# The opening of a two-layer Fourier and attention kernel: another order of its loads, turns and sine steps, written out by hand

## The chip, the cores and the metric

One core of a Trainium2 chip runs the whole program, all in fp32. The metric is device time in microseconds (us): the median of three runs of the kernel before is 1846.85 us (1846.19 to 1848.97). A profiled execution, from which every other number here comes, took 1846.4 us.

The engines are named as in the profile: PE is TensorE, DVE is VectorE, ACT is ScalarE, POOL is GpSimd, and SP is the engine whose queue issues most loads. Each engine works through its own instructions in a fixed order and waits at semaphores.

## The reference

Two layers on 256 tokens and 256 context tokens of width 2048. Both layers modulate a normalised input by vectors that come from a matrix product with `ada_w`. The first layer is a Fourier mixer with 16 groups of 256 channels:

```python
shift, scale, gate = jnp.split((jax.nn.silu(c) @ ada_w[i] + ada_b[i])[:, None, :], 3, axis=-1)
h = _rmsnorm(x, norm_g[i]) * (1 + scale) + shift
...
u, z = jnp.split(h @ w_in, 2, axis=-1)
ug = u.reshape(b, n, FNET_GROUPS, FNET_GROUP_DIM).astype(jnp.float32)
f = jnp.fft.fft2(ug, axes=(1, 3), norm='ortho').real.astype(h.dtype)
f = jnp.einsum('bngc,gcd->bngd', f, w_mix).reshape(b, n, D_BRANCH)
return f * jax.nn.silu(z)
...
x = x + gate * (y @ w_out[i])
```

The second layer is windowed attention with context keys and a sink, then a last norm. The change touches the first layer's opening alone.

## The kernel before

The kernel takes the Fourier transform over the tokens first, on the raw input, and multiplies by `w_in` afterwards. So the opening, roughly the first 130 us, has three strands of work:

- **Transform steps** (`x_split`, `dft_unit`, `evac_dft`): the 16 column blocks k of the input, 128 columns each, times cosine and sine tables. Each gives a tile `hx[k]`, which must then be scaled by the modulation (`scale_hx`, DVE line 286 and ACT line 285) and get its first column repaired (`fix_f0`), before it can be used.
- **Ada tiles** (`ada_tile`, PE line 213): 32 loads of 1 MiB, `awp`, each worth 8 matmuls in the trace. Four tiles make one row block: shift or scale for a quarter of the columns (four column blocks k). Its rows are copied out by ACT (`ada_rows`, line 218), and turned by four PE transposes, the "turns" (`ada_fin`, line 225), after which DVE adds the bias and stores shift or scale. Tiles 0 to 3 give the scale of the first quarter, 4 to 7 its shift, and so on to tile 31, the last shift.
- **Fill steps** (`fill_pe`, `u_step`, `sp_step`): products of the weights `wu` with the scaled `hx`, for groups 0, 1 and 2. The weights of a group come in two halves kh of 1 MiB, for column blocks 0 to 7 and 8 to 15. A half is folded by DVE into a difference (`m`, the sine part) and a sum (`p`, the cosine part); each is split into a high and a low number (ACT casts, line 62; DVE subtracts, line 63), since fp32 products are made of three matmuls (`mm3`, lines 75 to 77). A step (g, nm, k) is three matmuls; "s" is a product for two single columns of every group. The list `fill` fixes the order of the steps, `fill_pe(n)` takes the next n of them. Sine steps need no repaired column, cosine steps do.

Loads go through SP's queue, in the order of the program, into a few buffers (`raw_st` hands them out: three named raw, two raw2, two raw3); a load is issued when the matmuls or the fold that used its buffer before are done. Smaller loads go through ACT's queue. The third group's halves (g = 2) are loaded by `load_uh(2, kh, ...)` into raw2 buffers and folded by `fold_2`: the difference at line 463, the sum, in place, at line 460.

PE's order is chained by hand with `pe_next()`: what stands under it is issued behind the last matmul named `pe_end`. `tc.issue_after(x)` holds other work back to behind instruction x. What is not chained is ordered by a scheduler when the program is built. Before the change, a loop `for p in range(8, 12)` with `opening_step(p)` placed tiles 16 to 23 (two a step), and the tail, from `ada_tile(24)` on, was written out.

Within the loop `for g in range(G)` that follows (lines 535 to 616), PE goes on with group 0's mixing and then the groups up to 15.

Of the kernel before, what the change touches and what calls it, by code (L numbers as in the profile page):

```python
# [10 lines left out]
F32 = mybir.dt.float32  # L11
# [5 lines left out]
P = 128  # L17
D = 2048
KT = D // P
# [9 lines left out]
def tile_dit(ctx: ExitStack, tc: tile.TileContext, a: dict, out: bass.AP):  # L29
# [133 lines left out]
    with tc.tile_pool(name="st", reuse_waits="tile", bufs=1, side="right") as st:  # L163
# [111 lines left out]
            V.tensor_copy(f0[:, k, :], o[:, 0::N])  # L275
            hx.append(r)

        scale_end = [None]

        def scale_hx(k):  # L280
            r = hx[k]
            h, l = act(F32R), act(F32R)
            for s in range(2):
                q = slice(s * N, (s + 1) * N)
                S.activation(h[:, q], r[:, q], AF.Copy, scale=gs0[:, k, s : s + 1])
                scale_end[0] = V.scalar_tensor_tensor(l[:, q], r[:, q], gs0[:, k, s : s + 1], h[:, q].bitcast(F32), op0=ALU.mult, op1=ALU.subtract).ins
            hx[k] = (h.rearrange("p (s j) -> p s j", s=2), l.rearrange("p (s j) -> p s j", s=2))

# [27 lines left out]
        for g, nm, k in ((0, "m", 0), (0, "p", 0), (0, "m", 4), (1, "m", 0), (1, "p", 0), (1, "m", 4), (0, "p", 4), (1, "p", 4), (0, "s", 0), (0, "s", 4), (0, "m", 8), (1, "m", 8), (0, "p", 8), (1, "p", 8), (0, "s", 8), (2, "m", 0), (2, "m", 4), (0, "m", 12), (1, "m", 12), (2, "m", 8), (2, "m", 12), (2, "p", 0), (2, "p", 4), (2, "p", 8), (0, "p", 12), (0, "s", 12), (1, "p", 12), (2, "p", 12)):  # L316
# [11 lines left out]
        fills = {7: (8, 4), 11: (4, 0)}  # L328

        def opening_step(p):  # L330
            nb, which = p // 4, 1 - p // 2 % 2
            if p == 0:
                x_split(0)
            if p == 1:
                x_split(1)
            if p in (2, 4):
                x_split(p // 2 + 1, (0,))
            us_ = units.get(p, ())
            fl = fills.get(p, (4, 4))
            if p < 2:  # L340
# [30 lines left out]
            for k in range(KT):  # L371
                if max(k // 4 * 4 + 2, k // 2) == p:
                    scale_hx(k)
            if p % 4 == 0 and p:
                fix_f0(p // 4 - 1)

        uload = {4: (0, 0), 6: (1, 0), 7: (0, 1), 9: (1, 1)}
        uhold = {(0, 0): 4.9, (1, 0): 6.9, (0, 1): 7.9, (1, 1): 9.9}
        for p in range(5):
            opening_step(p)  # L380
        sta.close()
# [4 lines left out]
            wu[0][0] = split_uh(*raws[0, 0])  # L386
        opening_step(6)
        raws[1, 0] = fold_uh(raws[1, 0], 1, 0)
        opening_step(7)
        with tc.issue_after(rows_end[0]):  # L390
            wu[1][0] = split_uh(*raws[1, 0])
        del ring[5:]
        std.close()

# [26 lines left out]
            m_end[1] = V.scalar_tensor_tensor(sp[64:96, :], o2[64:96, 0:GD], mk[64:96, g : g + 1], sp[64:96, :].bitcast(F32), op0=ALU.mult, op1=ALU.subtract).ins  # L421
            return pqh, pql, sp

        for p in range(8, 12):
            if p == 8:
                cst = ua.tile([P, 4, P], F32, name="cst", bufs=1)
                nc.scalar.dma_start(cst, a["cst"])
                ch = ua.tile([P, 4, P], F32R, name="ch", bufs=1)
                cl = ua.tile([P, 4, P], F32R, name="cl", bufs=1)
                mk = cload("mk", [96, G], nc.scalar, adap)  # L430
                wsr = wsp.tile([P, 512], F32, tag="ws", name="wsr")
                nc.scalar.dma_start(wsr, a["wsp"])
            opening_step(p)
            if p == 9:
                split(ch, cl, cst)
                spw = wsp.tile([P, 1024], F32R, tag="ws", name="spw")
                sph, spl = spw[:, 0:512], spw[:, 512:1024]
                split(sph, spl, wsr)
                with pe_next(), tc.issue_after(f0_end[0]):
                    m0 = load_m(0)  # L440
            if p == 11:
                with pe_next():
                    m1 = load_m(1)
            for kh, q in ((0, 8), (1, 10)):
                if p == q:
                    raws[kh, 1] = fold_uh(raws[kh, 1], kh, 1)
                if p == q + 1:
                    with tc.issue_after(rows_end[0]):
                        wu[kh][1] = split_uh(*raws[kh, 1])

        def split_ws(nm, t):
            l = wsp.tile([P, 8, 127], F32R, tag="ws", name=f"w{nm}l")
# [4 lines left out]
        def fold_2(kh, nm):  # L457
# [5 lines left out]
            V.tensor_tensor(m, v[:, :, 0, :], v[:, :, 1, :], op=ALU.subtract)  # L463
            wu[2][kh]["m"] = split_ws("m", m)

        ada_tile(24)
        ada_tile(25)
# [903 lines left out]
```

## Time and profile before

| what | number |
|---|---|
| median of three runs | 1846.85 us |
| profiled execution | 1846.4 us, span from first to last instruction 1844.5 us |
| PE busy | 1812.6 us of the span |
| DVE, ACT busy | 1395.3 us, 958.1 us |
| DMA | 366.37 MB, 199 GB/s on the mean |
| loads of `awp` | 32 of 1 MiB, median 13.0 us from issue to landing |
| loads of `wu` | 32 of 1016 KB, median 8.0 us from issue to landing |

How to read the views that follow. A row of the stretches gives the window, its length, then the busy time of PE, PE's weight loads, DVE, ACT and POOL with counts, the granted TensorE clock, the mean busy share of the DMA engines and GB/s. A row of the timeline gives the start, the duration, engine, line, operation, output and inputs with buffer numbers left out, shapes, and how many like it were merged; in brackets the idle time before it and what ended it. A row of the waits gives who waited for whom: total us, times, longest. In DMA rows the queue of the issuing engine is named, SPq for example.

### The profile page before, as it was taken

To read this page: it belongs to the slowest core of one execution; us is meant where nothing else is said; L and a number is where in the kernel's file an instruction comes from. 1 tells how busy PE (TensorE), PEld (TensorE's weight loads), DVE (VectorE), ACT (ScalarE), POOL (GpSimd) and SP (SyncE) were. 2 spreads that over 40 slices of the span, in tenths; PEclk is the share of its full clock that TensorE was granted. 3 is DMA by queue.
4 is the path that set the end of the run, shared out by engine and by line. 5 is a ranking of instruction groups with operands and counts; after the bars stand their busy time and mean duration, and the time that the engine had idled before them with its cause. 6 is when DMAs were issued, how large, how long until landed. Compare 5 with 4: busy or idle time off the path is not lost.

```text
span 1844.5 us, 26534 instructions
## 1 busy us (share of the span) xinstructions
PE 1812.6 (98%) x9917; PEld 1548.5 (84%) x9917; DVE 1395.3 (76%) x2777; ACT 958.1 (52%) x1662; POOL 173.8 (9%) x185
## 2 busy tenths in 40 slices
PE   6999999999999999999999999999999999999997
PEld 5689999888888888888888888888888888888886
DVE  5688888787878887858874836878878878887455
ACT  5444444432222242214222625888888888897343
POOL 0001212000000000000000001121220220300001
PEclk9999999999999999999999999999999999999999
DMA  9988889666666648553575324333333333444553
GB/s 394 417 314 233 222 232 275 225 226 224 243 244 262 235 169 294 214 214 114 206 286 208 115 95 156 123 130 138 115 117 135 135 117 137 160 138 179 186 182 137
DMA packets 74593, 366.37 MB, mean 199 GB/s; under 512 B 21153, under 2 KB 21809, under 8 KB 39393
## 3 DMA queue, kind: packets, MB, share of 16 engines
q1 hardware_dynamic: 50400, 326.67, 48.2%
q0 software_dynamic: 19920, 31.06, 6.6%
q10 hardware_dynamic: 4144, 6.95, 1.2%
q8 instruction: 78, 1.28, 0.3%
q14 instruction: 51, 0.41, 0.1%
HBM read 352.06 MB, written 12.59 MB: 198 GB/s over the span
## 4 chain that ended last, share of the span: by engine, by line
PE 93%; DMA 3%; DVE 2%; ACT 1%; issue 1%; POOL 0%; POOLq 0%; SPq 0%; ACTq 0%; DVEq 0%
PE ps L75 24%; PE ps L76 24%; PE ps L77 24%; PE ps L1052 6%; PE ps L1054 3%; PE ps L1108 3%; DMA raw<-in_awp 2%; PE ps L1123 2%; PE ps L1122 2%; PE ps L1088 2%; PE ps L1089 2%; PE ps L213 1%; DMA raw<-in_wu 1%; PE ps L968 0%; DMA xn<-in_x 0%
## 5 line engine op out<-in xcount | busy, mean ns | idle before, releaser
L62 ACT CAST wh<-raw 128x1024 fp32r<-128x1024 f32 x333 | 349.9, 1052 | 548.7 <-PE ps L76 465.1
L63 DVE TENSOR_TENSOR wl<-raw,wh 128x1024 fp32r<-128x1024 f32 x333 | 421.9, 1269 | 231.3 <-ACT wh L62 228.2
L76 PE MATMUL ps<-act,wh 128*128 128x512 f32 x1024 | 398.2, 389 | 0.0
L75 PE MATMUL ps<-act,wh 128*128 128x512 f32 x1024 | 394.5, 389 | 0.0
L77 PE MATMUL ps<-act,wl 128*128 128x512 f32 x1024 | 392.8, 389 | 0.0
L77 PEld LDWEIGHTS ps<-act,wl 128*128 128x128 f32 x1024 | 192.2, 188 | 39.9
L76 PEld LDWEIGHTS ps<-act,wh 128*128 128x128 f32 x1024 | 192.2, 188 | 39.8
L75 PEld LDWEIGHTS ps<-act,wh 128*128 128x128 f32 x1024 | 192.2, 188 | 39.8
L1052 PE MATMUL ps<-h,wh 128*128 128x512 f32 x512 | 186.4, 399 | 0.0
L645 DVE CUSTOM_DVE_ANT_0 raw<-raw,cb 128x512 f32<-128x512 f32 x256 | 172.7, 689 | 9.5 <-DMA raw<-in_adw 5.8
L645 DVE CUSTOM_DVE_ANT_0 junk<-raw,cb 128x512 f32<-128x512 f32 x192 | 132.0, 687 | 32.1 <-DMA raw<-in_adw 20.3
L1054 PE MATMUL ps<-h,wl 128*128 128x256 f32 x512 | 138.2, 280 | 0.0
L76 PE MATMUL ps<-wl,h 128*128 128x512 f32 x320 | 125.4, 392 | 0.0
L77 PE MATMUL ps<-wh,h 128*128 128x512 f32 x320 | 124.2, 391 | 0.0
L75 PE MATMUL ps<-wh,h 128*128 128x512 f32 x320 | 123.6, 396 | 0.5 <-ACT h L859 0.5
L1052 PEld LDWEIGHTS ps<-h,wh 128*128 128x128 f32 x512 | 96.0, 188 | 18.4
L1090 DVE CUSTOM_DVE_ANT_0 ps<-ps,mask,nsink 128x512 f32<-128x512 f32 x128 | 92.1, 754 | 11.7 <-PE ps L1089 10.6
L1093 ACT ACTIVATE p<-ps,mx 128x512 f32<-128x512 f32 x128 | 87.4, 687 | 24.8 <-DVE mx L1090 24.2
L1054 PEld LDWEIGHTS ps<-h,wl 128*128 128x128 f32 x512 | 96.8, 189 | 1.4
L63 DVE TENSOR_TENSOR pl<-ps,ph 128x512 fp32r<-128x512 f32 x128 | 83.7, 685 | 9.8 <-ACT ph L62 9.0
L1098 ACT ACTIVATE p<-p,sm 128x512 f32<-128x512 f32 x128 | 85.4, 716 | 7.8 <-DVE sm L1096 7.8
L75 PE MATMUL ps<-act,wph 128*127 128x260 f32 x256 | 73.5, 287 | 1.1 <-DVE act L241 1.1
(321 smaller groups left out, 3578.8 us busy)
## 6 DMA issues: line engine op xcount, KB each, us to landing
raw<-in_wz SPq DMA_DIRECT2D x64, 1024.0 KB, 4.9
raw<-in_adw SPq DMA_DIRECT2D x64, 1024.0 KB, 5.1
raw<-in_awp SPq DMA_DIRECT2D x32, 1024.0 KB, 13.0
raw<-in_wo SPq DMA_DIRECT2D x32, 1024.0 KB, 5.3
raw<-in_wq SPq DMA_DIRECT2D x32, 1024.0 KB, 4.9
raw<-in_wu SPq DMA_DIRECT2D x32, 1016.0 KB, 8.0
raw<-in_wo1b SPq DMA_DIRECT2D x16, 1024.0 KB, 4.8
act<-in_xT POOLq DMA_DIRECT2D x32, 256.0 KB, 6.2
```

The costliest lines, as they stand in the source:

```text
L62: last_cast[0] = S.copy(h, src).ins
L63: last_sub[0] = V.tensor_tensor(l, src, h.bitcast(F32), op=ALU.subtract).ins
L75: PE.matmul(o, wh, xh, start=start, stop=False)
L76: PE.matmul(o, wh, xl, start=False, stop=False)
L77: return PE.matmul(o, wl, xh, start=False, stop=stop).ins
L645: V.tensor_tensor_reduce(junk if s == 0 and i < 3 else wf, wf, cb[:, s, kq * 512 : kq * 512 + 512], 1.0, 0.0, ALU.mult, ALU.add, acc[:, i, ...
L1052: PE.matmul(o[0], wh[:, q], hx1[k], start=k == 0, stop=k == KT - 1)
L1054: PE.matmul(o[0][:, 0:N], wl[:, q], hx1[k][:, 0:N], start=False, stop=False)
L1090: V.tensor_tensor_reduce(o, o, mask[:, tb, :], -0.125, nsink[:, i : i + 1], ALU.add, ALU.min, mx[:, tb : tb + 1])
L1093: S.activation(pt[:, tb, :], so[tb], AF.Exp, bias=mx[:, tb : tb + 1], scale=-1.0, accum_out=sm[:, tb : tb + 1])
L1098: S.activation(pt[:, tb, :], pt[:, tb, :], AF.Copy, scale=sm[:, tb : tb + 1])
L1108: PE.transpose(o[:, (kt * 2 + tb) * P : (kt * 2 + tb + 1) * P], pt[:, tb, c : c + P], ident)
```

## The change

It reorders the opening, and adds or removes no instruction on any engine.

- In `opening_step`, `ada_fin` of the row block before stands ahead of the step's two tiles, not behind them.
- The loop for p = 8 to 11 is written out. Fill steps stand between single tiles, mostly four, and the list `fill` is in another order: (0, "p", 4), (0, "s", 0), (2, "m", 0) and (2, "m", 4) stand earlier.
- The second group's halves are split in two parts, m and p, at places of their own; its second half is loaded behind tile 19.
- The third group's first half is loaded ahead of tile 24, not behind tile 25, its difference is folded behind tile 25, its sum behind tile 28. Its second half is still asked for behind tile 27; its folds are placed behind tile 29.

SP's loads, in the order of the built programs, from tile 19 on (w11 is group 1's second half, w20 and w21 are group 2's halves):

```
before: 19 w11 20 21 22 23 24 25 26 27 w20 28 w21 29 30 31
after:  19 20 w11 21 22 23 w20 24 25 26 27 28 29 30 w21 31
```

PE's order at the end of the opening (t is a tile, T the turns, a triple the four steps from k on):

```
before: t27 (0,s,8) T (2,m,0) t28 (2,m,4) t29 (0,m,12) (1,m,12) t30 t31 (2,m,8) T (2,m,12)
after:  t25 (2,m,0) t26 (1,p,8) t27 (2,m,4) T t28 (0,s,8) (0,m,12) t29 (1,m,12) t30 (2,m,8) t31 (2,m,12) T
both:   (2,p,0) (2,p,4) (2,p,8) (0,p,12) (0,s,12) (1,p,12) (2,p,12), then the loop over the groups
```

The core of the diff:

```diff
@@ opening_step
+            if pend:
+                ada_fin(*pend.pop())
             ada_tile(2 * p)
-            if p == 8:
-                fill_pe(4)
             ada_tile(2 * p + 1)
...
-            if pend:
-                ada_fin(*pend.pop())
...
-        for p in range(8, 12):
...
+        ada_fin(*pend.pop())
+        fix_f0(1)
+        with tc.issue_after(rows_end[0]), tc.issue_after(f0_end[0]):
+            wu[1][0]["p"] = split_part("p", raws[1, 0][0])
+        fill_pe(8)
+        ada_tile(16)
+        fill_pe(4)
+        with tc.issue_after(last_sub[0]):
+            raws[0, 1] = fold_uh(raws[0, 1], 0, 1)
+        ada_tile(17)
+        fill_pe(4)
...
+        ada_tile(18)
+        fill_pe(4)
+        ada_tile(19)
+        raws[1, 1] = load_uh(1, 1, raw_st, 9.9, 7)
+        rows = ada_rows()
+        wu[0][1] = split_uh(*raws[0, 1])
+        fill_pe(4)
+        ada_fin(2, 1, rows)
...
+        ada_tile(23)
+        rows = ada_rows()
+        fill_pe(2)
+        ada_fin(2, 0, rows)
+        fix_f0(2)
+        with tc.issue_after(f0_end[0]):
+            wu[1][1]["p"] = split_part("p", raws[1, 1][0])
...
+        v2 = [load_uh(2, 0, raw_st, 20, 5, "raw2")]
         ada_tile(24)
+        fill_pe(4)
         ada_tile(25)
-        v2 = [load_uh(2, 0, raw_st, 20, 5, "raw2")]
-        ada_fin(*pend.pop())
-        fill_pe(4)
-        fix_f0(2)
+        with tc.issue_after(last_sub[0]):
+            fold_2(0, "m")
         fill_pe(4)
         ada_tile(26)
         fill_pe(4)
         ada_tile(27)
         v2.append(load_uh(2, 1, raw_st, 20, 5, "raw2"))
-        with tc.issue_after(f0_end[0]):
-            fold_2(0, "m")
-            fold_2(0, "p")
-        with tc.issue_after(last_cast[0]):
-            rows = ada_rows()
+        rows = ada_rows()
         fill_pe(4)
         ada_fin(3, 1, rows)
         for k in range(12, KT):
             scale_hx(k)
+        ada_tile(28)
+        fold_2(0, "p")
+        fill_pe(8)
+        ada_tile(29)
+        fold_2(1, "m")
+        fold_2(1, "p")
         fill_pe(4)
-        ada_tile(28)
+        ada_tile(30)
         fill_pe(4)
-        ada_tile(29)
-        fill_pe(8)
-        ada_tile(30)
         ada_tile(31)
         rows = ada_rows()
-        with tc.issue_after(scale_end[0]):
-            fold_2(1, "m")
-            fold_2(1, "p")
```

More of the change, by code (lines that the diff above doesn't have):

```diff
@@ L276, in evac_dft @@
             hx.append(r)
-        scale_end = [None]
+        scale_end, scale_act = [None], [None]
         def scale_hx(k):
@@ L315, in tile_dit @@
         fill = []
-        for g, nm, k in ((0, "m", 0), (0, "p", 0), (0, "m", 4), (1, "m", 0), (1, "p", 0), (1, "m", 4), (0, "p", 4), (1, "p", 4), (0, "s", 0), (0, "s", 4), (0, "m", 8), (1, "m", 8), (0, "p", 8), (1, "p", 8), (0, "s", 8), (2, "m", 0), (2, "m", 4), (0, "m", 12), (1, "m", 12), (2, "m", 8), (2, "m", 12), (2, "p", 0), (2, "p", 4), (2, "p", 8), (0, "p", 12), (0, "s", 12), (1, "p", 12), (2, "p", 12)):
+        for g, nm, k in (
[3 rows of a table added]
+        ):
             fill += [(g, nm, k + i) for i in range(4)]
@@ L370, in opening_step @@
                 fill_pe(fl[1])
-            for k in range(KT):
-                if max(k // 4 * 4 + 2, k // 2) == p:
+            for k in range(8):
+                if k // 4 * 4 + 2 == p:
                     scale_hx(k)
@@ L388, in tile_dit @@
         raws[1, 0] = fold_uh(raws[1, 0], 1, 0)
+        with tc.issue_after(scale_act[0]):
+            wu[1][0] = {"m": split_part("m", raws[1, 0][1])}
         opening_step(7)
-        with tc.issue_after(rows_end[0]):
-            wu[1][0] = split_uh(*raws[1, 0])
         del ring[5:]
@@ L422, in load_m @@
             return pqh, pql, sp
-        for p in range(8, 12):
[L425 to L449, printed above, removed]
@@ new lines, in tile_dit @@
+        cst = ua.tile([P, 4, P], F32, name="cst", bufs=1)
+        nc.scalar.dma_start(cst, a["cst"])
+        ch = ua.tile([P, 4, P], F32R, name="ch", bufs=1)
+        cl = ua.tile([P, 4, P], F32R, name="cl", bufs=1)
+        mk = cload("mk", [96, G], nc.scalar, adap)
+        wsr = wsp.tile([P, 512], F32, tag="ws", name="wsr")
+        nc.scalar.dma_start(wsr, a["wsp"])
+        ada_fin(*pend.pop())
+        fix_f0(1)
+        with tc.issue_after(rows_end[0]), tc.issue_after(f0_end[0]):
+            wu[1][0]["p"] = split_part("p", raws[1, 0][0])
@@ new lines, in tile_dit @@
+        fill_pe(8)
[5 more added lines that the diff above has]
+        fill_pe(4)
+        split(ch, cl, cst)
+        spw = wsp.tile([P, 1024], F32R, tag="ws", name="spw")
+        sph, spl = spw[:, 0:512], spw[:, 512:1024]
+        split(sph, spl, wsr)
+        ada_tile(18)
[3 more added lines that the diff above has]
+        rows = ada_rows()
@@ new lines, in tile_dit @@
+        wu[0][1] = split_uh(*raws[0, 1])
+        fill_pe(4)
+        ada_fin(2, 1, rows)
+        for k in range(8, 12):
+            scale_hx(k)
+        with pe_next(), tc.issue_after(f0_end[0]):
+            m0 = load_m(0)
+        fill_pe(4)
+        ada_tile(20)
+        with tc.issue_after(scale_end[0]):
+            raws[1, 1] = fold_uh(raws[1, 1], 1, 1)
+        fill_pe(4)
+        ada_tile(21)
+        with pe_next():
+            m1 = load_m(1)
+        with tc.issue_after(scale_act[0]):
+            wu[1][1] = {"m": split_part("m", raws[1, 1][1])}
```

11 lines of the change are left out of this document (7 added, 4 removed), and 3 rows, old and new, of the table fill.

## The prediction

> **What bounds the kernel now.** I read the page first: busy shares and the chain that ended last.
>
> ```profile
> span 1844.5 us, 26534 instructions
> ...
> PE 1812.6 (98%) x9917; PEld 1548.5 (84%) x9917; DVE 1395.3 (76%) x2777; ACT 958.1 (52%) x1662; POOL 173.8 (9%) x185
> ...
> PE 93%; DMA 3%; DVE 2%; ACT 1%; issue 1%; POOL 0%; POOLq 0%; SPq 0%; ACTq 0%; DVEq 0%
> ```
>
> TensorE (PE) sets the end. The changed kernel has exactly the same instructions on every engine as before; only their order in the opening (the first 135 us or so) differs. So only PE's idle time can change. Next I read the busy time by stretch; in each row the second number is the length and the third is PE's busy time.
>
> ```profile
> 0.00:10.00 10.00, 0.00 (x0) 0.00 (x0) 2.19 (x9) 3.99 (x5) 1.78 (x10) 1.00 0.79 304
> ...
> 20.00:60.00 40.00, 38.88 (x324) 28.02 (x320) 22.60 (x65) 23.22 (x45) 0.00 (x0) 1.00 1.01 419
> 60.00:70.00 10.00, 8.16 (x61) 5.04 (x60) 8.59 (x13) 4.64 (x8) 0.00 (x0) 1.00 1.02 411
> 80.00:90.00 10.00, 7.69 (x52) 4.43 (x50) 8.70 (x20) 4.16 (x10) 0.00 (x0) 1.00 1.02 419
> 90.00:100.00 10.00, 8.90 (x71) 5.41 (x71) 4.87 (x16) 3.31 (x5) 0.00 (x0) 1.00 1.01 419
> 100.00:110.00 10.00, 10.00 (x83) 6.80 (x85) 7.05 (x14) 4.94 (x10) 0.00 (x0) 1.00 1.01 403
> 110.00:120.00 10.00, 10.00 (x84) 7.58 (x84) 8.11 (x21) 4.27 (x9) 0.75 (x1) 1.00 0.97 374
> 120.00:130.00 10.00, 10.00 (x84) 9.86 (x83) 9.92 (x16) 6.04 (x10) 1.51 (x1) 1.00 0.57 145
> 150.00:1840.00 1690.00, 1681.98 (x8907) 1448.52 (x8905) 1292.52 (x2533) 882.09 (x1523) 163.78 (x165) 1.00 0.53 184
> ```
>
> The last two numbers are the DMA share and GB/s. Up to about 115 us the DMA engines are full (share 1.0 at about 420 GB/s): a transfer of 1 MiB takes 1.0486 MB / 420 GB/s = 2.50 us, and they come one behind the other. PE's gaps between 20 and 100 us (1.1 + 1.8 + 2.3 + 1.1 in the rows shown) are waits for work that this stream feeds. From 100 to 130 us PE has no gap, and behind 150 us only 8 in 1690. Hence a microsecond won or lost at the point where the opening's work joins the main loop stays won or lost to the end.
>
> **The point that decides.** Everything behind the last ada tile (31) is the same sequence in both kernels, but one block of 12 matmuls: (2,m,8..11), the third group's sine steps on its second weight half, stands behind tile 31 before and ahead of it after the change. I compare the start of the final block (group 2's cosine steps, the first matmul on wph below), since from there PE's order is the same up to small swaps in the first loop rounds.
>
> ```profile
> 109.95 1.07 PE L213 MATMUL ps<-raw,c 128*32 128x512 f32 x8
> 110.94 0.38 PE L75 MATMUL ps<-act,wmh 128*127 128x256 f32 x1
> ...
> 114.01 1.92 PE L213 MATMUL ps<-raw,c 128*32 128x512 f32 x16
> 115.86 0.38 PE L75 MATMUL ps<-act,wmh 128*127 128x256 f32 x1
> ...
> 117.37 0.60 PE L225 MATMUL ps<-ident,rows 128*128 128x128 f32 x4
> 117.73 0.36 PE L75 MATMUL ps<-act,wmh 128*127 128x256 f32 x1
> ...
> 119.23 0.28 PE L75 MATMUL ps<-act,wph 128*127 128x260 f32 x1
> ```
>
> Units of work from these rows: one tile alone 0.99, and 1.07 with the hand-over to it; 12 sine steps 117.37 - 115.86 = 1.51 right behind a tile, or 10 matmuls in 1.2; four transposes 0.36. Before, tiles 30 and 31 run together from 114.01 and the final block starts at 119.23.
>
> **The change part by part.** (a) Loads. SP issues the same loads in another order; the rows before are:
>
> ```profile
> 92.15 0.33 SPq L192 DMA_DIRECT2D raw<-in_wu  x1
> 94.53 0.33 SPq L46 DMA_DIRECT2D raw<-in_awp  x1
> 95.39 0.33 SPq L192 DMA_DIRECT2D raw<-in_wu  x1
> 101.39 7.42 SPq L46 DMA_DIRECT2D raw<-in_awp  x3
> ```
>
> These are group 2's first half, tile 28, group 2's second half, tiles 29, 30, 31. Behind the change the first half goes four places earlier (ahead of tile 24), tiles 24 to 27 one place later each (2.5 us), tile 28 stays, tiles 29 and 30 go one place earlier, and the second half goes two places later, between tiles 30 and 31. The total up to tile 31 stays, so with a full stream tile 31 lands when it did. VectorE (DVE) shows when the first half landed, because it had waited for it:
>
> ```profile
> 97.39 0.19 DVE L229 TENSOR_REDUCE sh<-ps 128x8 f32<-128x32 f32 x1
> ...
> 98.51 0.37 DVE L242 TENSOR_TENSOR act<-f,act 128x2 fp32r<-128x2 f32 x4
> 101.62 1.22 DVE L463 TENSOR_TENSOR wm<-raw 128x1016 f32<-128x1016 f32 x1 [2.74 <-DMA raw<-in_wu]
> 102.88 1.22 DVE L460 TENSOR_TENSOR raw<-raw 128x1016 f32<-128x1016 f32 x1
> 104.01 1.21 DVE L63 TENSOR_TENSOR wml<-wm,wmh 128x1016 fp32r<-128x1016 f32 x1
> ...
> 107.21 3.28 DVE L286 SCALAR_TENSOR_TENSOR act<-act,gs 128x256 fp32r<-128x256 f32 x8 [0.38 <-ACT act L285]
> 110.41 1.21 DVE L463 TENSOR_TENSOR wm<-raw 128x1016 f32<-128x1016 f32 x1
> ```
>
> So that place lands at 101.6. After the change it is tile 27's; three earlier tile 24 at 94.1, then tile 25 at 96.6, tile 26 at 99.1; the second half lands four later, at 101.6 + 4 x 2.50 = 111.6, and tile 31 at 114.1 or a little later (a small load of another queue joins in; before, PE took it at about 114.9, the middle of the 114.01 row).
>
> (b) Turns first. The four transposes of a finished row block (L225) move ahead of the next tile's matmuls. Cost on PE nothing (same instructions); the tile behind them is 0.4 later and its buffer is freed 0.4 later. Cover: the loads stand in a queue for longer than that (13.0 us from issue to landing, the last number of the page's row). If that cover failed it would cost 0.4 once per row block.
>
> ```profile
> raw<-in_awp SPq DMA_DIRECT2D x32, 1024.0 KB, 13.0
> ```
>
> (c) Fill order and the spacing of fill between single tiles. From tile 14 on there were 12 runs of tile matmuls, six of them pairs; now there are 16, two of them pairs. A broken pair costs 2 x 0.99 - 1.85 = 0.13 and a hand-over of 0.08: 4 x 0.21 = 0.8. It lies ahead of the deciding point, and its cover is the wait found in (d); without that cover it costs 0.8. PE's waits for tiles, 3.7 us in five, lie ahead of that point too.
>
> ```profile
> PE ps L213 <- DMA raw<-in_awp: 3.7, 5, 1.3
> ```
>
>
> (d) The new wait, worked out step by step in the changed order. Tile 23 keeps its place, 101.6 - 5 x 2.50 = 89.1, and PE took it at about 91.1 before (second half of a run of two at 90.17); I take 90.1.
>
> ```profile
> 90.17 1.92 PE L213 MATMUL ps<-raw,c 128*32 128x512 f32 x16
> ...
> 105.40 0.60 PE L225 MATMUL ps<-ident,rows 128*128 128x128 f32 x4
> ```
> ```profile
> 102.93 1.04 ACT L62 CAST wmh<-wm 128x1016 fp32r<-128x1016 f32 x1 [7.41 <-DVE wm L463]
> 104.11 0.59 ACT L218 COPY rows<-ps 128x512 f32<-128x512 f32 x1
> ```
>
> Tile, row copy and turns put DVE at 92.3. DVE then has, in this order, the modulation fix (97.39 to 98.88, 1.5), a split of group 1 (1.13), the fold of group 2's first half (1.26), the in-place add (1.13) and the subtract (1.21): low weights at 98.6. PE's third matmul of (2,m,0) waits for them: block done 99.9; tile 26 and 12 steps 102.5; tile 27 and 12 steps 105.0; turns; tile 28 106.5; 12 single-column steps 107.9. The steps (0,m,12) need the scaled rows, whose last is 110.41 - 105.40 = 5.0 behind the start of the turns, here 110.0; that block ends at 110.5, tile 29 at 111.6, (1,m,12) at 113.0, tile 30 at 114.1. PE now wants the second half.
>
> The cast (1.04) of the first half's cosine weights needs the buffer that (0,m,12) frees at 110.4, and DVE's split of it stands ahead of the second half's fold: 110.5 + 1.04, then 1.13, gives 112.8. The fold is done at 114.05, the cast for the high weights 114.1 to 115.15; the in-place add to 115.2; the subtract to 116.45. ScalarE (ACT) and DVE thus give PE its third matmul at 116.55, where it stood from 114.1 on. Queued behind on PE: ten matmuls (117.75), then tile 31, which has long landed (118.85), 12 steps (120.35), turns (0.36): the final block at 120.7. Against 119.23 that is **+1.5 us**. Nothing else is late: behind the last turns DVE needs 1.5, against a final block of 36 matmuls at 0.12, 4.4 us.
>
> Bounds. If DVE and ACT took the second half the moment it landed, the low weights would be there 1.1 earlier (+0.4). If the block were already done when tile 31 comes, the final block would start 1.5 earlier than before, 12 steps less behind the same tile: **-1.5**, the floor that the stream sets. Above: a transfer lost from the stream costs 2.5 on top, **+4.0**. I take +1.5, since each term has a row of the same operation and shape.
>
> [...] If the second half and tile 31 shared the stream to the end, the half would land at about 114.1 and the sum would be +4.0; what this trace says for strict order is the fold at 101.62, which began on the first half while two later loads (issued at 94.53 and 95.39) were under way.
>
> **Rivals.** A, the waits go and none comes: PE reaches the deciding block early enough, because the 3.7 us of tile waits are gone and the fold is quick. -1.5 to 0, so about 1845.7. For it: the largest gaps stand at 80 to 90 us, where the fill is respaced. Against it: the second half lands 5 us later than before (111.6, not 106.6), while tile 31 can't land earlier.
>
> B, slower by over 0.2%: the stream runs dry. The second half goes into a buffer that tile 27's matmuls free (done at 103.6 in my count). A load took about 6 us from issue to landing at the stream's end (the last of the three issues above ends at 101.39 + 7.42 = 108.8, tile 31 was taken at 114.9), so the issue must come before 105.5. If PE is over 1.9 us later than counted at tile 27, each further microsecond is lost; at a whole place the half lands at 114.1, and the final block is 2.5 later again: +4.0, so 1850.9, and more if more is late. For it: (2,m,0) ahead of tile 26 hangs on five DVE operations in a row. Against it: 1.9 us of slack, and a full stream before.
>
> [...]
>
> ```profile
> 18.59 0.41 PE L75 MATMUL ps<-dh,xh 128*128 128x256 f32 x1
> 18.80 0.41 PE L76 MATMUL ps<-dl,xh 128*128 128x256 f32 x1
> ...
> 22.44 0.28 PE L75 MATMUL ps<-dh,xh 128*128 128x256 f32 x1
> 22.56 0.28 PE L76 MATMUL ps<-dl,xh 128*128 128x256 f32 x1
> ```
>
> After the idle start the same matmul came every 0.21 us, from 22 us on every 0.12. [...]
>
> C, the change doesn't do what it says: DVE and ACT, not the order of loads, hold PE, and the old gaps only move. 0, so 1846.9.
>
> **How the numbers follow.** The profiled execution took 1846.4 us (span 1844.5); its sum is 1846.4 + 1.5 = 1847.9. The median of the runs is 0.45 higher, 1846.85 + 1.5 = 1848.35, say 1848.4. Chances: forecast (+0.4 to +3) 0.55, A 0.11, B 0.24, C 0.10. A measurement of this kernel tells about 0.2%, 3.7 us, from no change (the three runs themselves spread over 2.8 us). Forecast, A and C lie within it, up to 0.03 for A beyond its floor, and most of B beyond 1850.5, together with the forecast's upper tail: faster 0.03, same 0.68, slower 0.29. The range goes from A, 1845.3, to a little over B, 1851.9; the forecast's own range is 1847.2 to 1849.9.
>
> **What would show it.** In the changed profile: PE waits, within (2,m,8..11) between tiles 30 and 31, first for the high weights, then about 1.0 us for the low ones; the fold of the second half starts near 112.8 behind the split of the first half; tile 31's matmuls start near 117.8; the final block near 120.7; the stream stays full to 114. A wait of 0.5 to 1 us for low weights shows also at (2,m,0) near 98. I am wrong if tile 31's matmuls start before 116 (A), if the second half lands after 113 or the DMA share falls below 0.95 between 100 and 110 us (B), or if PE's gaps behind 130 us differ between the two.

## The result, and the profile after

The changed kernel takes 1850.16 us in the median of 20 runs (1847.32 to 1851.98), the kernel before 1846.36 (20 runs, 1845.64 to 1849.87). The ratio of the times is 1.0016, with a 95% interval of 1.0010 to 1.0023: 3.0 us slower (1.8 to 4.2). The two medians themselves lie 3.8 us apart; all comparisons below go by the ratio. By it the change is inside the 0.2% that the prediction called no change, and clear of the noise. The profiled execution took 1850.99 us with a span of 1849.0, 4.5 us over the span before.

The chain of the opening's end in the changed kernel, from TensorE's timeline (start, duration, engine and line, operation, tiles, count; in brackets the idle time before it and what ended it):

```profile
114.19 1.07 PE L213 MATMUL ps<-raw,c 128*32 128x512 f32 x8
116.10 0.39 PE L75 MATMUL ps<-act,wmh 128*127 128x256 f32 x1 [0.84 <-ACT wmh L62]
116.33 0.28 PE L76 MATMUL ps<-act,wmh 128*127 128x256 f32 x1
117.41 0.38 PE L77 MATMUL ps<-act,wml 128*127 128x256 f32 x1 [0.81 <-DVE wml L63]
117.63 0.28 PE L75 MATMUL ps<-act,wmh 128*127 128x256 f32 x1
117.75 0.28 PE L76 MATMUL ps<-act,wmh 128*127 128x256 f32 x1
117.87 0.35 PE L77 MATMUL ps<-act,wml 128*127 128x256 f32 x1
118.02 0.41 PE L75 MATMUL ps<-act,wmh 128*127 128x256 f32 x1
118.23 0.41 PE L76 MATMUL ps<-act,wmh 128*127 128x256 f32 x1
...
119.43 1.94 PE L213 MATMUL ps<-raw,c 128*32 128x512 f32 x8
121.30 0.39 PE L75 MATMUL ps<-act,wmh 128*127 128x256 f32 x1
...
122.85 0.60 PE L225 MATMUL ps<-ident,rows 128*128 128x128 f32 x4
123.20 0.37 PE L75 MATMUL ps<-act,wph 128*127 128x260 f32 x1
```

The two waits of the forecast are there, between tiles 30 and 31: 0.84 us for the high weights, then 0.81 for the low ones. But then something else shows: from 118.02 on matmuls that came every 0.12 us come every 0.21 to 0.22, and tile 31 takes 1.94 us and not 1.07. The final block starts at 123.20, where it started at 119.23 before.

VectorE and ScalarE of the same execution, ahead of these waits:

```profile
107.80 3.29 DVE L286 SCALAR_TENSOR_TENSOR act<-act,gs 128x256 fp32r<-128x256 f32 x8 [0.38 <-ACT act L285]
112.64 1.22 DVE L63 TENSOR_TENSOR wpl<-raw,wph 128x1016 fp32r<-128x1016 f32 x1 [1.55 <-ACT wph L62]
113.77 1.21 DVE L492 TENSOR_TENSOR wm<-raw 128x1016 f32<-128x1016 f32 x1
115.01 1.22 DVE L489 TENSOR_TENSOR raw<-raw 128x1016 f32<-128x1016 f32 x1
116.15 1.21 DVE L63 TENSOR_TENSOR wml<-wm,wmh 128x1016 fp32r<-128x1016 f32 x1
```
```profile
111.56 1.04 ACT L62 CAST wph<-raw 128x1016 fp32r<-128x1016 f32 x1 [0.99 <-PE ps L76]
115.01 1.04 ACT L62 CAST wmh<-wm 128x1016 fp32r<-128x1016 f32 x1 [2.41 <-DVE wm L492]
```

The cosine split (wpl) waits for its cast, which waits for the buffer, and stands ahead of the fold (L492): fold at 113.77, low weights at 117.36, TensorE 0.05 later.

The granted clock shows only in narrow windows of the changed kernel (start and end; length; then busy us and instructions of TensorE, its weight loads, VectorE, ScalarE, GpSimd; the granted clock; DMA share; GB/s). On the 40 slices of the profile's page it is 9 tenths throughout.

```profile
111.11:114.52 3.41, 3.38 (x26) 2.10 (x30) 1.88 (x2) 1.04 (x1) 0.24 (x1) 1.00 0.88 300
114.52:117.94 3.42, 1.77 (x14) 0.82 (x7) 3.36 (x4) 2.08 (x2) 0.00 (x0) 1.00 1.00 397
117.94:121.35 3.41, 3.41 (x17) 1.52 (x16) 0.67 (x1) 0.00 (x0) 0.00 (x0) 0.50 0.43 179
121.35:124.76 3.41, 3.41 (x32) 3.41 (x30) 1.14 (x11) 1.23 (x6) 0.00 (x0) 1.00 0.66 222
```

Within the opening TensorE ran at half clock for exactly one stretch of 3.41 us, right behind the window that holds both waits. At 0.213 us per matmul in place of 0.118 that costs 3.41 x (1 - 0.118 / 0.213) = 1.5 us.

**Where the 4.5 us of the two profiled executions lie.** Comparing the same matmul of both traces by its number: this execution is already 0.58 later at TensorE's 300th matmul record (54 us), where little of the change has come; I put that down to the start of an execution, not to the change (e9 below, the same kernel, is 0.24 later there). At the final block it is 123.20 - 119.23 = 3.97 later, so the opening cost 3.39: 1.5 by the clock, and 1.9 that is left for the waits. The last 0.5 comes between 220 and 450 us, where TensorE has a wait that the profile of the kernel before doesn't show:

```profile
255.25 0.39 PE L76 MATMUL ps<-ml,ch 128*128 128x256 f32 x1 [1.03 <-DVE ml L63]
```

Between 220 and 450 us e2 and e3 below, in which TensorE's order behind the opening is that of the changed kernel, gain 0.6 and 0.9 us on the profile before and have no such wait. In e9, the same kernel once more, it comes to 1.8 us, and in e5, which has the order of the kernel before there, to 2.2. So it differs from execution to execution, and I don't count it to the change.

TensorE's waits over the whole changed kernel, by what ended them (us in total, times, longest):

```profile
PE ps L213 <- DMA raw<-in_awp: 1.6, 3, 1.0
PE ps L77 <- DVE wml L63: 1.6, 2, 0.8
...
PE ps L75 <- ACT mh L62: 0.9, 1, 0.9
PE ps L75 <- ACT wmh L62: 0.8, 1, 0.8
```

Waits for tiles fell from 3.7 us to 1.6, as the respaced fill promised. Against that stand waits for low weights, 1.6 in two (0.8 in one before), for the high ones, 0.8, and one of 0.9 for the cast `mh`, near 89 us, where the kernel before has none. The other wait for low weights is the forecast's small one, at (2,m,0):

```profile
99.42 0.38 PE L77 MATMUL ps<-act,wml 128*127 128x256 f32 x1 [0.75 <-DVE wml L63]
```

### The profile page after: what moved, and what is told of

Its sections match the earlier page's. It is cut to its first block, busy times and chain, and to the rows that moved or that the text cites. A ratio compares the mean times of both kernels' runs of the same rounds, so it can differ in the third digit from the quotient of the medians.

```text
span 1849.0 us, 26539 instructions
## 1 busy us (share of the span) xinstructions
PE 1815.2 (98%) x9917; PEld 1548.2 (84%) x9917; DVE 1394.3 (75%) x2777; ACT 958.2 (52%) x1662; POOL 173.0 (9%) x185
## 4 chain that ended last, share of the span: by engine, by line
PE 92%; DMA 3%; DVE 2%; ACT 1%; issue 1%; POOL 0%; POOLq 0%; SPq 0%; DVEq 0%; ACTq 0%
PE ps L75 24%; PE ps L76 24%; PE ps L77 24%; PE ps L1077 6%; PE ps L1079 3%; PE ps L1133 3%; DMA raw<-in_awp 2%; PE ps L1148 2%; PE ps L1147 2%; PE ps L1113 2%; PE ps L1114 2%; DMA raw<-in_wu 1%; PE ps L213 1%; PE ps L993 0%; ACT wh L62 0%
## 5 line engine op out<-in xcount | busy, mean ns | idle before, releaser
L76 PE MATMUL ps<-wl,ys 128*128 128x512 f32 (+1 forms) x192 | 74.4, 388 | 0.0
```

What stands on the lines that cost most here:

```text
L76: PE.matmul(o, wh, xl, start=False, stop=False)
```

## The experiments

The experiments weigh three theories, by which the expectations are told. Theory 1: the loss is the wait at (2,m,8..11) for the third group's late second half, plus the half clock that this wait brings about. Theory 2: it lies in the rest of the new order (turns first, single tiles with fill between them). Theory 3: the wait costs, the half clock is chance. Besides its run times against the kernel before (on the same chip, 11 runs and more, 8 and 5 for the two with the repeated fold) each run is read by its final block: its start less 119.23, and less that execution's own lead or lag at the 300th matmul record ("opening"). This reading takes it that the lead carries through; the two profiled executions of the changed kernel differ by 0.3 in it, so a few tenths mean nothing. In e4, e8, e10 and e12 the scheduler also changed the order of some instructions of a much later stage, near 380 us; the opening's number is free of that. There is one profile of each run, and no run e6.

| run | against before, us (95%) | final block | opening, us | half clock in the opening |
|---|---|---|---|---|
| changed kernel | +3.0 (+1.8 to +4.2) | 123.20 | +3.4 | 117.94, 3.41 us |
| e9, changed again | +3.1 (+1.5 to +4.8) | 123.12 | +3.7 | 117.38, 3.41 us |
| e1, half early | +1.3 (-0.4 to +3.0) | 120.30 | +0.9 | none |
| e2, fold first | +0.6 (-0.9 to +2.2) | 119.67 | +0.6 | none |
| e3, 16 matmuls more | +2.0 (+0.4 to +3.7) | 121.33 | +2.1 | none |
| e11, 6 matmuls more | +1.3 (-0.4 to +3.0) | 120.98 | +2.1 | none |
| e4, tile in the wait | +0.7 (-0.9 to +2.4) | 120.06 | +0.7 | none |
| e5, turns first alone | +0.2 (-1.5 to +1.8) | 120.82 | +1.0 | 89.51, 3.41 us |
| e7, fold twice | +4.8 (+3.0 to +6.6) | 122.52 | +3.0 | none |
| e8, fold thrice | +6.8 (+4.4 to +9.2) | 126.66 | +7.1 | 119.07, 6.83 us |
| e10, reordered | +1.3 (-0.4 to +2.8) | 120.21 | +1.1 | 88.32, 3.41 us |
| e12, casts kept | -0.2 (-1.8 to +1.5) | 119.34 | +0.2 | none |

**e1: the late half loaded early.**

```diff
+        v2.append(load_uh(2, 1, raw_st, 20, 5, "raw2"))
         ada_tile(27)
-        v2.append(load_uh(2, 1, raw_st, 20, 5, "raw2"))
```

> The changed kernel with one edit: the load of the third group's second half is issued ahead of tile 27 and not behind tile 30, so tiles 27 to 30 land one place later and the half four places earlier (about 111.9 - 4 x 2.5 = 101.9 us). TensorE's order is untouched. Theory 1 (the change loses 1.5 us in the waits of (2,m,8..11) for the late half and 1.5 us in the half clock that follows them): both waits go, no stretch at half clock, the final block starts near 119.6 where it started at 123.2, total 0 us against the kernel before (-1 to +0.7). Theory 2 (the loss comes from the rest of the reorder: single tiles with fill between them, or turns first): the total stays at +3 us (+1.8 to +4.2). Theory 3 (the wait alone costs, the half clock was a chance of the profiled execution): as theory 1 here.

VectorE and TensorE of this run:

```profile
101.57 1.22 DVE L492 TENSOR_TENSOR wm<-raw 128x1016 f32<-128x1016 f32 x1 [2.65 <-DMA raw<-in_wu]
```
```profile
104.08 1.07 PE L213 MATMUL ps<-raw,c 128*32 128x512 f32 x8 [1.00 <-DMA raw<-in_awp]
```

The fold starts at its landing, 101.57 us, twelve microseconds earlier than in the changed kernel, and both waits at (2,m,8..11) are gone, with them the half clock. Of the 3.4 us of the opening 2.5 come back. Theory 2 would have kept all of the loss. The run came out at +1.3 and not at 0, though: tile 27, whose load went one place back, is now late, and TensorE waits 1.00 for it.

**e2: the fold ahead of the cosine splits.**

```diff
+        late = last_cast[0], last_sub[0]
         fill_pe(4)
         ada_tile(30)
...
-            wu[2][kh]["p"] = split_part("p", v2[kh][:, :, 0, :])
+            with tc.issue_after(late[0]), tc.issue_after(late[1]):
+                wu[2][kh]["p"] = split_part("p", v2[kh][:, :, 0, :])
```

> The changed kernel with one edit: the split of the third group's cosine weights, both halves, may start only behind the cast and the subtract that make the second half's sine weights; loads and TensorE's order are untouched. Theory 1 (late landing, then the cosine split standing ahead of the fold on VectorE): the fold starts at the landing, about 112.0 and not 113.8, the low weights are there at about 115.7 and not 117.4, TensorE waits 0.2 to 0.4 us in place of 1.65, and the clock is not halved: 1.65 + 1.5 = 3.1 us less than the changed kernel, 0 us against the kernel before (-1 to +0.7). Theory 2 (the loss comes from elsewhere in the reorder): +3 us against before. Theory 3 (wait alone, no clock): 1.65 less than the changed kernel, about +1.4.

VectorE, then TensorE:

```profile
111.78 1.22 DVE L492 TENSOR_TENSOR wm<-raw 128x1016 f32<-128x1016 f32 x1 [0.97 <-DMA raw<-in_wu]
113.04 1.22 DVE L489 TENSOR_TENSOR raw<-raw 128x1016 f32<-128x1016 f32 x1
114.17 1.21 DVE L63 TENSOR_TENSOR wml<-wm,wmh 128x1016 fp32r<-128x1016 f32 x1
```
```profile
114.91 0.38 PE L75 MATMUL ps<-act,wmh 128*127 128x256 f32 x1
115.13 0.28 PE L76 MATMUL ps<-act,wmh 128*127 128x256 f32 x1
115.43 0.39 PE L77 MATMUL ps<-act,wml 128*127 128x256 f32 x1
```

The half lands as late as ever, at 111.76 us (111.94 in the changed kernel), but is folded at once, and TensorE takes the low weights at 115.43 and not at 117.41, with next to no wait. There is no half clock, and the opening falls from +3.4 to +0.6. So the late landing alone costs little, about the +0.4 that the prediction's lower bound had for a half taken at its landing: what made the wait is the cosine split that stood ahead of the fold. Loads and TensorE's order are those of the changed kernel here, so by the opening about 0.6 is left for theory 2; the interval of the median reaches +2.2.

**e3 and e11: the wait kept, TensorE kept busy.** 16 matmuls, and in e11 6, whose result nobody reads:

```diff
         ada_tile(30)
+        with pe_next():
+            o = psum()
+            h, l = hx[0]
+            for i in range(16):
+                r = PE.matmul(o[0:127, 0:256], wu[0][1]["p"][0][:, 0, :], h[:, :, 128:256], start=True, stop=True)
+        pe_end[0] = r.ins
         fill_pe(4)
```

> The changed kernel with 16 matmuls more, of 0.118 us each, whose result nobody reads, on TensorE between tile 30 and (2,m,8..11): 1.9 us of work where TensorE waited 0.84 and 0.81 us. The late half stays late. Theory 1 (waits 1.5 us plus 1.5 us of half clock which the waits bring about): no stretch at half clock near 118 us in the profile, the final block near 121.8 and not 123.2; the total falls by 1.2 us (0.7 to 1.5) against the changed kernel although there is more to do, so +1.6 us against before (+0.8 to +2.5). Theory 3 (the half clock does not belong to the waits): the total stays, or rises by up to 0.3 us: +3 us against before, and the half-clock stretch may come as before. Theory 2 says the same as theory 3.

> The changed kernel with 6 matmuls more (not 16) of 0.118 us, whose result nobody reads, between tile 30 and (2,m,8..11): 0.7 us of work inside the first wait of 0.84 us, so the weights are not taken later. Theory 1, in its sharper form (the clock is halved for 3.41 us behind each window of 3.41 us in which matmuls streamed for less than about 0.40 of the time; the changed kernel's window had 0.34 to 0.39, and 6 matmuls add 0.21): no stretch at half clock near 118 us, the final block at about 121.7, total +1.9 us against before (+1 to +3), 1.1 us less than the changed kernel. Theory 3 (the half clock does not hang on how much TensorE does in the window): halved as often as the changed kernel, +3.0 us, the final block at 123.2 in a halved execution.

TensorE in e3, then in e11:

```profile
114.85 2.16 PE L523 MATMUL ps<-act,wph 128*127 128x256 f32 x16
116.85 0.28 PE L75 MATMUL ps<-act,wmh 128*127 128x256 f32 x1
```
```profile
114.47 0.97 PE L523 MATMUL ps<-act,wph 128*127 128x256 f32 x6
116.72 0.38 PE L77 MATMUL ps<-act,wml 128*127 128x256 f32 x1 [0.80 <-DVE wml L63]
118.09 1.06 PE L213 MATMUL ps<-raw,c 128*32 128x512 f32 x8
```

With more work for TensorE the opening is 1.3 us shorter, twice: +2.1 in place of +3.4 (and +3.7 in e9). Less each execution's own lead, the weights come no earlier: the low ones are done at 117.0 or 117.1, and at 116.8 in the changed kernel. In e11 the second wait stands untouched, 0.80, and tile 31 behind it takes 1.06, at full clock. So in both profiles the half clock is gone with the waits filled, and its price in the opening (1.3 here, 1.5 there) is about what the sum gave it. One profile each does not rule out chance (theory 3); the last section sets the windows of the profiles side by side. The run times go the same way (+2.0 and +1.3 for +3.0), but their intervals overlap with that of the changed kernel, so they don't settle it.

**e4: tile 31 ahead of (2,m,8..11).**

```diff
-        fill_pe(4)
         ada_tile(31)
+        fill_pe(4)
```

> The changed kernel with one edit: tile 31's matmuls stand ahead of (2,m,8..11), as they did in the kernel before, and fill the wait with their 1.07 us. Theory 1: TensorE takes tile 31 at about 115.3, then waits about 0.9 us for the low weights (117.4), the final block starts near 120.4; if that single wait leaves the clock alone the total is 0.6 us above before (0 to +1.2), with a stretch at half clock +2.1. Theory 2 (single tiles, turns first): +3 us against before, since these parts stay. Theory 3: 1.0 us less than the changed kernel, +2.0.

TensorE waits only once, 0.81 for the low weights at 117.00, and there is no half clock. Opening and run times are both at +0.7, as theory 1 has it.

**e5: turns first alone**, on the kernel before:

```diff
+            if pend:
+                ada_fin(*pend.pop())
             ada_tile(2 * p)
...
-            if pend:
-                ada_fin(*pend.pop())
```

> The kernel before with one part of the change: the four transposes of a finished row block go ahead of the next tile's matmuls, in the steps of the opening. Theory 1 (all of the loss lies at (2,m,8..11)): 0 us against before (-0.7 to +0.7). Theory 2 (a part of the remaining 0.5 us of the opening, which is left when the late half's waits are gone, comes from the turns): +0.3 to +1 us, seen in the profile as later matmuls behind the turns of the opening.

The run times are those of the kernel before. The profiled execution had a stretch at half clock of its own, at 89.51, so its opening of +1.0 is about -0.5 without it: these runs show no cost of turns first, within an interval that reaches +1.8. These are its windows, columns as above:

```profile
86.09:89.51 3.42, 2.44 (x14) 1.53 (x11) 3.42 (x9) 3.06 (x8) 0.00 (x0) 1.00 1.01 417
89.51:92.92 3.41, 3.31 (x16) 1.10 (x19) 0.33 (x1) 0.00 (x0) 0.00 (x0) 0.50 1.03 420
```

**e7 and e8: the wait made longer.** The fold of the second half is computed twice (e7) and three times (e8) over:

```diff
+            for _ in range(2 if kh else 1):
-            V.tensor_tensor(m, v[:, :, 0, :], v[:, :, 1, :], op=ALU.subtract)
+                V.tensor_tensor(m, v[:, :, 0, :], v[:, :, 1, :], op=ALU.subtract)
```

> The changed kernel, with the fold of the third group's second half (1.21 us on VectorE) computed twice over, so that the low and high weights come 1.2 us later and TensorE's waits at (2,m,8..11) grow from 1.65 to about 2.85 us. Theory 1 (the clock is halved for 3.41 us when the waits in one window of 3.41 us come to about 1.6 us; the windows run freely against the kernel, so both waits of the changed kernel fell whole into one window in 8 of 20 runs): now nearly 9 runs of 10 are halved, listed at a mean clock of 0.997; +1.2 us of wait and 0.5 x 1.5 us of clock more than the changed kernel: +5.0 us against before (+4 to +6). Theory 3 (the half clock comes by chance, whatever the wait): the share of halved runs stays at 4 of 10, +4.2 us.

> The same fold computed three times over: waits of about 4.05 us in all at (2,m,8..11). Theory 1: every run has a stretch at half clock, some of them two (6.8 us), since the waits are longer than a window; +2.4 us of wait and 0.9 to 2 us of clock more than the changed kernel: +6.5 us against before (+5.5 to +8). Theory 3: 4 of 10 runs halved, +5.4 us.

TensorE in e7, its windows, and the windows of e8:

```profile
116.97 0.39 PE L75 MATMUL ps<-act,wmh 128*127 128x256 f32 x1 [2.10 <-ACT wmh L62]
118.28 0.38 PE L77 MATMUL ps<-act,wml 128*127 128x256 f32 x1 [0.80 <-DVE wml L63]
```
```profile
112.84:116.25 3.41, 2.04 (x17) 0.99 (x15) 3.34 (x4) 0.37 (x1) 0.00 (x0) 1.00 0.93 337
116.25:119.67 3.42, 1.89 (x16) 1.55 (x16) 3.20 (x3) 1.72 (x2) 0.00 (x0) 1.00 0.83 340
119.67:123.08 3.41, 3.41 (x29) 2.57 (x29) 0.24 (x2) 1.23 (x6) 0.00 (x0) 1.00 0.37 88
```
```profile
115.66:119.07 3.41, 0.51 (x2) 0.30 (x2) 3.34 (x4) 1.61 (x2) 0.00 (x0) 1.00 1.00 398
119.07:122.49 3.42, 2.89 (x14) 2.41 (x18) 1.69 (x2) 0.47 (x1) 0.00 (x0) 0.50 0.03 10
122.49:125.90 3.41, 3.41 (x17) 2.01 (x10) 0.00 (x0) 1.23 (x6) 0.00 (x0) 0.50 0.24 43
```

Both differences are near what theory 1 gave (+4.8 for +5.0, +6.8 for +6.5). e7's profiled execution is the instructive one: its first wait grew from 0.84 to 2.10, by 1.26, and its clock stayed at 1.00. The end of a window parts its waits (at 116.25), and in the two windows that hold them TensorE was busy for 2.04 and 1.89 us. Its opening of +3.0 less 1.26 is 1.7: the price of the changed kernel's waits without the clock, got a second way (1.9 above). In e8 the wait fills a whole window, and two stretches follow. How many of a kernel's runs are halved no run shows: the mean clock listed with a run, which the expectations of e7 and e9 lean on, mixes in the half clock at the end of the run (0.50 in the profile before from 1838.4 us to its last instruction at 1844.5), and e9's profiled execution, which had the stretch, is listed at 0.998, as is the profile before, which had none.

**e9: the changed kernel again.**

> The changed kernel once more, unaltered, on the chip of the three runs beside it. Theory 1: +3.0 us against before (+1.8 to +4.2), of which 1.5 us in about 4 runs of 10, those listed at a mean clock of 0.997; where the profiled execution has no stretch at half clock, its final block starts at about 121.2 and not 123.2.

+3.1, and the profiled execution had the stretch again, from 117.38 us and not from 117.94.

**e10 and e12: a better order.** e10 is e2 with two more edits; e12 is e10 with ScalarE's cast kept at its place.

```diff
-        with tc.issue_after(f0_end[0]):
-            wu[1][1]["p"] = split_part("p", raws[1, 1][0])
...
-        with tc.issue_after(last_sub[0]):
+        with tc.issue_after(f0_end[0]):
             fold_2(0, "m")
+        with tc.issue_after(last_cast[0]), tc.issue_after(last_sub[0]):
+            wu[1][1]["p"] = split_part("p", raws[1, 1][0])
...
-        fill_pe(4)
         ada_tile(31)
+        fill_pe(4)
```

and in e12, against e10:

```diff
+            wpl = wfp.tile([P, 8, 127], F32R, tag="wf", name="wpl")
+            wph = wfp.tile([P, 8, 127], F32R, tag="wf", name="wph")
+            S.copy(wph, raws[1, 1][0])
...
-        with tc.issue_after(last_cast[0]), tc.issue_after(last_sub[0]):
-            wu[1][1]["p"] = split_part("p", raws[1, 1][0])
+        with tc.issue_after(last_sub[0]):
+            V.tensor_tensor(wpl, raws[1, 1][0], wph.bitcast(F32), op=ALU.subtract)
+        wu[1][1]["p"] = wph, wpl
```

> The changed kernel with three edits: the cosine split of the third group behind the fold of its second half (as in the run with the fold first); the cosine split of group 1's second half behind the fold of the third group's first half, so that TensorE's wait of 0.8 us at (2,m,0) goes; tile 31's matmuls ahead of (2,m,8..11), so that TensorE has work until the low weights are there (about 115.4). Theory 1: from the landing of tile 31 (114.4) on TensorE has no wait, final block at about 114.4 + 1.0 + 24 x 0.12 + 0.4 = 118.7 against 119.2 before, no stretch at half clock there, total -0.5 us against before (-1.5 to +0.5). Theory 2 (something else in the new order of tiles and sine steps costs the 0.6 us that were left over): +0.6 us against before, final block at about 119.8.

> As the run before it with three edits (cosine split of the third group last, VectorE's subtract of group 1's cosine split behind the fold of the third group's first half, tile 31 ahead of (2,m,8..11)), but ScalarE keeps the order of its casts, so that the wait for the cast mh at 88 us stays at 0.9 us and is not 2.1 us. Theory 1: no window under 0.40 in the opening, no stretch at half clock; no wait at (2,m,0) nor at (2,m,8..11); tile 31 is taken at its landing, about 114.5; final block at about 118.7 against 119.2 before; total -0.5 us against before (-1.5 to +0.5). Theory 2 (the new order of tiles and sine steps has a price of its own): +0.6 to +1 us, final block at 119.7 or later.

e10 missed. TensorE, and the window behind its wait:

```profile
87.94 0.39 PE L75 MATMUL ps<-mh,ch 128*128 128x256 f32 x1 [2.08 <-ACT mh L62]
```
```profile
84.91:88.32 3.41, 1.33 (x10) 0.32 (x9) 3.41 (x6) 1.66 (x2) 0.00 (x0) 1.00 1.02 424
88.32:91.74 3.42, 3.42 (x17) 1.70 (x16) 0.65 (x2) 0.00 (x0) 0.00 (x0) 0.50 0.99 408
```

Moving the cosine split took its cast along on ScalarE, and the scheduler then put the matmul that needs mh ahead of a tile: a wait of 0.9 became 2.08, and the clock was halved behind it. e12 moves only VectorE's subtract:

```profile
113.39 1.06 PE L213 MATMUL ps<-raw,c 128*32 128x512 f32 x8
115.06 1.07 PE L213 MATMUL ps<-raw,c 128*32 128x512 f32 x8 [0.60 <-DMA raw<-in_awp]
...
119.34 0.37 PE L75 MATMUL ps<-act,wph 128*127 128x260 f32 x1
```

No wait for the third group's weights is left, tile 31 is taken as it lands, and the kernel is level with the one before: 1846.39 against 1846.42 us, ratio 0.9999 (0.9990 to 1.0008). It beats the changed kernel, not the one before: tile 31 landed at 115.0, not at 114.4 as expected, and what stands behind it is 12 matmuls more than the floor of -1.5 in the prediction has (the prediction calls them 12 steps). What is left for theory 2, the order of tiles and steps, is this +0.2 of the opening; the median's interval is -1.8 to +1.5.

## Why the prediction was right, and what it left out

- *The deciding point.* Right. The place (between tiles 30 and 31), the queue (cosine split ahead of the fold) and the order of the waits (high weights, then low) are those of step (d). Fold at 113.77 (forecast 112.8), TensorE's third matmul at 117.41 (116.55), each about 0.9 late; 0.6 of that is the start of the execution, and 0.1 a slip in the forecast's 112.8, whose terms add to 112.7. e2 shows that the split's place is the cause.
- *Its size.* The waits cost 1.7 to 1.9 us (two ways, above), forecast +1.5. Tile 31 and the final block came at 119.43 and 123.20 and not at 117.8 and 120.7; the difference is the start of the execution and the next point.
- *The term that the sum does not have: the clock.* The forecast's +1.5 counts the waits alone. The profiles showed 1.5 us more of half clock behind just these waits, with matmuls 0.21 us apart, as in the prediction's rows from the start of the execution: both profiled executions of the changed kernel have it (from 117.94 and from 117.38), and e3 and e11 don't, though their weights come no earlier. With it the forecast's sum is +3.0, against +3.4 and +3.7 in the openings of these two executions. How much of the +3.0 in the run times is the clock stays open, since no run shows how many of the executions were halved.
- *The number.* The forecast was +1.5 and the run times say +3.0. The median, 1850.16, lies above the forecast's own range, 1847.2 to 1849.9, and within the whole range only because that was drawn up to 1851.9 for rival B, which did not occur. That part is luck.
- *(a) Loads.* Right. In the trace of the changed kernel the half landed at 111.94 (forecast 111.6) and tile 31 at 114.43 (114.1 or a little later). All 64 loads of `awp` and `wu` on SP's queue landed in the order of their issue in this trace, at least 2.46 us apart, and in that of the kernel before, at least 2.47 apart.
- *(b) Turns first: 0.* Nothing speaks against it (e5, +0.2, -1.5 to +1.8).
- *(c) Single tiles: 0.8, covered.* No cost of it is left to see: e12 has nearly the same single tiles (30 and 31 run together) and stands at +0.2. The wait at (2,m,0) is there, 0.75 at 99.42 (forecast 0.5 to 1 near 98).
- *Same order behind the opening.* Not quite: a few matmuls near 150 to 170 us and later casts and subtracts are swapped too. The distance of the two traces stays there (4.0 us at 148 us, 3.9 at 233). Behind that the prediction's last sign of being wrong did show: TensorE's gaps behind 130 us differ, by the wait of 1.03 at 255.25. That the two are alike behind the opening thus didn't hold for this pair of executions; as e2, e5 and e9 show, that wait comes and goes with either order.
- *The rivals.* A (no wait) was what the change could have had with another order on VectorE: e2 and e12 come near its upper end, 0, and none is clearly below. B did not occur: its marks, a landing after 113 and a DMA share under 0.95 between 100 and 110 us, are missing (111.94, and a share of 1.01), and the half was asked for at 104.6, ahead of B's limit of 105.5. Its size, 4.0, is close to the 3.4 of the profiled opening, by another mechanism. C's time, 0, is out, but not its first half: e2 leaves the loads late and loses little, so it was the order on VectorE that held TensorE.

## What to carry to other kernels

When a load is moved earlier or later, follow its data through every engine's queue to the consumer: here the landing was 5 us later at a cost of about 0.6 us (e2), and an instruction that nobody needed yet, placed ahead of the fold, made the wait. Price a wait of TensorE for itself, and look for half clock behind it: here the two waits cost 1.7 to 1.9 us, and the 3.41 us at half clock behind them 1.5 more. Another tile in that place (e4), or even a few matmuls that nobody needs (e11), cost less than the wait with the half clock behind it. Look at the granted clock in narrow windows, since this stretch of 3.41 us didn't show in the 40 slices of the profile's page. Compare more than one execution: the wait of 1.03 us at 255.25 came and went between profiles here.

## What the runs showed of the hardware

The clock was halved without an idle window. In the changed kernel's trace the clock rises to full at 18.95 us (matmuls come every 0.21 us before it and every 0.12 behind it), and the stretch at half clock begins at 117.94, 98.99 us later: 29 times its own length of 3.413 us. Cut each trace into windows of that length, counted from where its clock first rises to full. TensorE's work in a window can be estimated from its timeline: 0.118 us for each matmul that begins in the window (a row of sine steps has them 0.12 apart) and 0.124 for each of the 8 records of a tile (0.99 / 8, from the prediction's units). The changed kernel's window from 114.52 then holds 4 x 0.124 + 6 x 0.118, the last one cut off by the window's end: 1.15 us, a share of 0.34. Seven windows, with TensorE's busy time and records from the profile:

| window | busy, us (records) | share, estimate | granted clock behind it |
|---|---|---|---|
| e8, from 115.66 | 0.51 (2) | 0.07 | 0.50 for 6.83 us |
| e10, from 84.91 | 1.33 (10) | 0.21 | 0.50 for 3.41 us |
| changed kernel, from 114.52 | 1.77 (14) | 0.34 | 0.50 for 3.41 us |
| e9, from 113.96 | 1.77 (14) | 0.37 | 0.50 for 3.41 us |
| e5, from 86.09 | 2.44 (14) | 0.40 | 0.50 for 3.41 us |
| kernel before, from 63.45 | 1.98 (13) | 0.415 | 1.00 |
| e7, from 116.25 | 1.89 (16) | 0.42 | 1.00 |

Up to 1830 us the changed kernel has no other window under 0.48 by this estimate, and the kernel before none under 0.415. The estimate was found in hindsight on the first runs; the expectation of e11 then gave "about 0.40", and neither e11 nor e12 had half clock in the opening. The nearest pair is a close call: e5's window and that of the kernel before both hold 12 matmuls, and only the one that the window's end cuts off sets them apart. So the share sorts these seven windows, and that it is what sets the clock was not shown. TensorE's busy time does not sort them: e5's window was busy for 2.44 us of 3.42 and was followed by half clock, e7's for 1.89 and was not. A record lasts longer than the matmul's share of the stream: in the changed kernel 0.28 us in a row of matmuls 0.12 apart, and 0.38 or 0.39 behind a wait.

The stretches at half clock were 3.41 us long, and 6.83 in e8. The windows ahead of them held 2 to 14 matmul records, so none was without a matmul. The windows do not keep their place against the matmuls: the two waits lie in one window in the changed kernel (114.52 to 117.94), and a window's end parts them in e7 (at 116.25). Why e8's clock stayed at half for a second window, in which TensorE was busy for 2.89 of 3.42 us, is open; no run was made for it.
